# A third gate pair ahead of an output projection, more low parts by accumulating DMA, an earlier load: one layer of a streaming encoder on one core

## The chip, the cores and the metric

The kernel runs on 1 core of a Trainium2 chip. The metric is the time of one execution on the device in microseconds (us); lower is better. The core's engines work side by side, each on its own queue of instructions: TensorE (PE in the profile; its weight loads are PEld), VectorE (DVE), ScalarE (ACT), GpSimd (POOL) and SyncE (SP), which here only issues DMAs. DMAs are also issued from POOL's and ScalarE's queues.

## What is computed

One layer with three branches over a normed input, 512 prompt rows and 64 sample rows of width 1024 (576 columns in the kernel's transposed layout), all in float32:

```
h = rmsnorm(x);  proj = h @ w_in
glu_v, glu_g, conv_gate, z, xbc, dt, q, xa_gate, gates = split(proj)
A: u = glu_v * sigmoid(glu_g); c = causal depthwise conv of u, width 31
   out_a = (silu(layernorm(c)) * silu(conv_gate)) @ conv_out_w
B: state-space scan (SSD) over conv4(xbc) with dt, 4 groups of 8 heads
   y = y * silu(z); y = y * rsqrt(mean(y*y) per group) * ssd_norm_w
   out_b = y @ ssd_out_w
C: k, v = rmsnorm(mem) @ xa_kv_w          (256 memory rows)
   4 heads: o = softmax(q k' / 16) v;  out_c = (o * silu(xa_gate)) @ xa_out_w
m = sum over the branches of sigmoid(gates + gate_b) * out
y = x + rmsnorm(m @ w_out)
```

The sample rows attend to cached k and v and use cached conv and scan states. New caches and states are outputs too.

## The kernel before

**Products in three passes.** Each float32 operand is held as a high part and a low part (value minus high part), both in float32r. A product takes three matmuls: high by high, high by low, low by high (`mac`, L209 to L217). A projection (`proj`, L221) of 128 output channels over 576 columns has 8 chunks of the contraction, three passes and two column halves: 48 matmuls. The activation's parts, `hT`, stay in the core for the whole run.

**Weight jobs.** Weights come as jobs of 512 KB in a list, `order` (L95 to L165), in the sequence in which TensorE uses them. `prep_to` (L172) prepares job by job: SP loads `raw`; ScalarE writes the high part `whi` (L189); the low part `wlo` is made in one of two ways. For jobs ahead of `hold`, and for names that begin with k or v, VectorE subtracts (L191). For the others ScalarE writes the negated value (L193) and a DMA from POOL's queue adds `raw` onto it (L194). There are 3 buffers each of `raw`, `whi` and `wlo` in the pool `wp`. `W(name)` (L204) asks for the preparation of two jobs more (`LA`) than the one that it returns. `hold` marks where preparation stops until the attention is reached (`limit`).

**Stages.** (1) Norm and transposes of the input. (2) SSD, four groups of five chunks; the projections of the next things stand between the chunks as fill. (3) The end of group 3: `gating_a(3)` squares and sums y; then come the conv branch's gates `glu(0)`, the norm `gating_b(3)` (L644: two small matmul pairs, a square root, a reciprocal of 576 columns, four products L657, four splits into parts L616 and L618), `glu(1)`, sums for the next stage, and `out_b(3, q)`, which adds the last group's 192 matmuls onto `ob`. `glu(2)` stands behind it. A `glu` (L743) is two projections, a tanh into a tile `t`, and a product on VectorE into a padded tile `u` (`u_tile`), with small POOL copies (L736 to L740). (4) Paired products: 17 pairs of projections are done with seven products instead of eight on half blocks (`slot`, L950; P1 to P7, 84 matmuls a pair). The combinations T1 to T4 of the activation for it are formed ahead (L768 to L797) in tiles `xp` and `acc`. `pair_load`, `pair_pure` and `pair_sum` prepare weights; `pair_pure` uses the accumulating DMA (L877). Pair 0 and pairs 5 to 8 are gates of the conv branch, pairs 1 to 4 the merge gates of branch B, whose products end in `ob` and are stored to `msc` (L944), pairs 9 to 12 the attention's gates (stored to `spill["xg"]`), pairs 13 to 16 the merge gates of branch C. (5) Attention, head by head: `att_kq` projects k and q, `att_k` writes k out, `att_scores` projects v, writes it out and makes the scores and the softmax; the next head's `att_kq` stands between a head's scores and `att_pt` (transposes of the softmax, L1174) and `att_out`. (6) From 890 us: the output projection of C, layernorm, the branch A, the merges, `w_out`.

**Taps in the background.** The conv of width 31 is 8 channel tiles of a first product on ScalarE (L809) and 30 taps on VectorE (L816), queued in `bg`. `bgrun(n)` takes n of them from the queue. In the paired products it is called with 1 after every second slot; in the attention and later at fixed places.

**The memory rows** are loaded by SP into columns of `ob` (`obf`) that pairs 1 to 4 have stored, and normed in place (`mem_prep`, L1002), both called in the loop ahead of slot P5 of pair 8. The squares' output goes to columns 2048 to 3071 of the same tile.

**Who sets the order.** The program order is the source's, but the framework schedules: it simulates a time line with its own costs and lets ready instructions of an engine pass others, by a priority that follows the source order; `bgrun` shifts the priority of taps by 150. Each engine then runs its instructions strictly in the sequence fixed so. Waits between engines, and on buffers being freed, are put in by the framework.

## Time and profile before

| | us |
|---|---|
| runs | 1141.45, 1140.26, 1145.55 (median 1141.45) |
| profiled execution | 1143.13 |
| its span in the trace | 1141.4 |
| mean granted TensorE clock | 0.986 |
| TensorE busy | 1097.9 (96%) |
| VectorE busy | 868.8 (76%) |
| ScalarE busy | 606.4 (53%) |
| POOL busy | 148.3 (13%) |

A row of the windows gives, for a stretch of the span, each engine's busy time and instruction count, then the clock granted to TensorE (1.00 is full), the mean busy share of the 16 DMA engines, and GB/s. A row of the timeline gives start, duration, engine, source line, operation, output <- inputs, shapes, and in brackets the idle time before it with what ended it. A row of a group ends with busy time and the mean in ns of one instruction. A row of waits gives who waited for whom: us in total, times, longest.

### The profile page before, as it was taken

The page shows a single profiled execution, that of the slowest core. Times are in us where ns is not written, and L with a number is a line of the kernel's source. Part 1 is how long each engine was busy: PE and PEld are TensorE (multiplying, and loading weights), DVE is VectorE, ACT ScalarE, POOL GpSimd, SP SyncE. Part 2 cuts the span into 40 slices and gives each one's busy share as a digit, 9 for nine tenths or more (in the row PEclk, how much of TensorE's full clock was granted, in tenths as well). Part 3 has the DMA queues.
Part 4 walks back from the last instruction along what each step waited for, and adds up shares of the span by engine and source line. Part 5 has one row for each costly group of instructions (what it writes and reads, how often), then busy time and mean ns, then how long its engine had stood idle before and what let it go on. Part 6 is the DMA issues. An engine that isn't in the chain of part 4 may idle for free.

```text
span 1141.4 us, 20485 instructions
## 1 busy us (share of the span) xinstructions
PE 1097.9 (96%) x8081; PEld 1052.2 (92%) x8081; DVE 868.8 (76%) x1371; ACT 606.4 (53%) x1065; POOL 148.3 (13%) x237
## 2 busy tenths in 40 slices
PE   8999999999999999599989999899999999999997
PEld 8999999999999999599989999899898999999974
DVE  5778898488969886946787887389999998685433
ACT  5665655464537432535676666474457234685331
POOL 0100110020002100313224321000001011111000
PEclk9999999999999999799999999999999999999999
DMA  7354423442443323167887887666567786788812
GB/s 204 94 169 130 126 83 107 123 113 79 116 115 99 93 63 100 37 144 153 209 198 158 182 211 198 180 161 167 147 161 185 206 208 150 160 180 196 230 45 83
DMA packets 201495, 164.55 MB, mean 144 GB/s; under 512 B 14935, under 2 KB 175743, under 8 KB 201399
## 3 DMA queue, kind: packets, MB, share of 16 engines
q1 hardware_dynamic: 187142, 126.55, 38.8%
q0 software_dynamic: 13104, 34.35, 16.7%
q10 hardware_dynamic: 1152, 2.36, 0.5%
q8 instruction: 63, 1.03, 0.4%
q14 instruction: 34, 0.27, 0.1%
HBM read 114.85 MB, written 14.03 MB: 113 GB/s over the span
## 4 chain that ended last, share of the span: by engine, by line
PE 84%; DVE 7%; issue 3%; DMA 3%; ACT 2%; POOL 0%; DVEq 0%; SPq 0%; ACTq 0%; POOLq 0%
PE mm L214 55%; PE X L905 7%; DVE c L816 3%; PE Y L905 3%; PE ps L214 3%; PE Z L905 2%; PE ps L1114 2%; PE ps L1115 2%; PE ps L1113 2%; DMA pl<-rawb 2%; PE ps L573 2%; PE ps L599 2%; PE ps L577 1%; DVE wlo L191 1%; PE ps L538 1%
## 5 line engine op out<-in xcount | busy, mean ns | idle before, releaser
L214 PE MATMUL mm<-hT,whi 128*128 128x288 f32 (+2 forms) x2240 | 397.3, 297 | 1.0 <-ACT ob L668 0.5
L214 PEld LDWEIGHTS mm<-hT,whi 128*128 128x128 f32 x2240 | 334.3, 189 | 3.4 <-issue 1.3
L214 PE MATMUL mm<-hT,wlo 128*128 128x288 f32 (+2 forms) x1120 | 246.4, 298 | 0.0
L189 ACT ACTIVATE whi<-raw 128x1024 fp32r<-128x1024 f32 x118 | 124.8, 1057 | 216.2 <-PE mm L214 169.1
L816 DVE SCALAR_TENSOR_TENSOR c<-u,dww,c 128x606 f32<-128x606 f32 x240 | 199.6, 846 | 2.8 <-ACT c L809 0.3
L214 PEld LDWEIGHTS mm<-hT,wlo 128*128 128x128 f32 x1120 | 184.8, 189 | 1.3 <-issue 0.7
L191 DVE TENSOR_TENSOR wlo<-raw,whi 128x1024 fp32r<-128x1024 f32 x78 | 95.2, 1221 | 51.2 <-ACT whi L189 50.8
L214 PE MATMUL mm<-hi,whi 128*128 128x288 f32 x512 | 112.3, 301 | 10.8 <-DVE xs L657 10.8
L214 PE MATMUL mm<-lo,whi 128*128 128x288 f32 x512 | 111.4, 298 | 3.8 <-DVE lo L618 3.8
L214 PE MATMUL mm<-hi,wlo 128*128 128x288 f32 x512 | 110.9, 297 | 0.0
L214 PEld LDWEIGHTS mm<-hi,whi 128*128 128x128 f32 x512 | 83.3, 191 | 12.2 <-ACT hi L616 11.0
L214 PEld LDWEIGHTS mm<-lo,whi 128*128 128x128 f32 x512 | 83.3, 190 | 4.4 <-DVE lo L618 4.4
L214 PEld LDWEIGHTS mm<-hi,wlo 128*128 128x128 f32 x512 | 83.2, 189 | 0.2 <-issue 0.2
L194 POOL DMA_DIRECT2D wlo<-raw x40 | 34.7, 868 | 329.9 <-ACT wlo L193 257.4
L466 DVE SCALAR_TENSOR_TENSOR acc<-xp,scw,acc 128x579 f32<-128x579 f32 x72 | 58.3, 815 | 3.1 <-ACT acc L462 1.9
L193 ACT ACTIVATE wlo<-raw 128x1024 fp32r<-128x1024 f32 x40 | 42.0, 1049 | 27.8 <-PE ps L214 27.8
L888 DVE TENSOR_TENSOR wlo<-sm,whi 128x1024 fp32r<-128x1024 f32 x34 | 41.5, 1222 | 12.1 <-ACT whi L887 11.9
L875 ACT ACTIVATE ph<-rawb 128x512 fp32r<-128x512 f32 x34 | 21.4, 631 | 49.9 <-PE X L905 37.5
L877 POOL DMA_DIRECT2D pl<-rawb x34 | 29.9, 887 | 96.7 <-ACT pl L876 71.3
L458 POOL COPY tails<-xp 128x3 f32<-128x3 f32 x24 | 17.3, 720 | 193.3 <-ACT xp L456 187.8
L887 ACT ACTIVATE whi<-sm 128x1024 fp32r<-128x1024 f32 x34 | 35.8, 1055 | 11.4 <-PE X L905 7.5
L559 ACT ACTIVATE M<-R,tok 128x128 f32<-128x128 f32 (+1 forms) x80 | 24.8, 380 | 12.3 <-PE ps L599 12.3
(375 smaller groups left out, 2277.8 us busy)
## 6 DMA issues: line engine op xcount, KB each, us to landing
raw<-in_w_in_dram SPq DMA_DIRECT2D x70, 512.0 KB
wlo<-raw POOLq DMA_DIRECT2D x40, 512.0 KB, 5.7
raw<-in_w_in_dram SPq DMA_DIRECT2D x34, 256.0 KB
rawb<-in_w_in_dram SPq DMA_DIRECT2D x34, 256.0 KB
pl<-rawb POOLq DMA_DIRECT2D x34, 256.0 KB, 4.7
R<-scr SPq DMA_DIRECT2D x16, 512.0 KB
raw<-in_ssd_out_w_dram SPq DMA_DIRECT2D x16, 512.0 KB
raw<-in_xa_kv_w_dram SPq DMA_DIRECT2D x16, 512.0 KB
```

The source lines that it names most:

```text
L189: a = nc.scalar.activation(hi[:, :n_], raw[:, :n_], AF.Copy)
L191: b = nc.vector.tensor_tensor(lo[:, :n_], raw[:, :n_], hi[:, :n_].bitcast(F32), ALU.subtract)
L193: nc.scalar.activation(lo[:, :n_], raw[:, :n_], AF.Copy, scale=-1.0)
L194: nc.gpsimd.dma_start(out=lo[:, :n_], in_=raw[:, :n_], accum_op=ALU.add)
L214: m = nc.tensor.matmul(o, lhsT=w, rhs=r[:, s:s + w_], start=(i == 0 and a == 0), stop=(i == n - 1 and a == 2),)
L466: nc.vector.scalar_tensor_tensor(acc, xp[:, r:r + 579], w4[:, r, jt:jt + 1], acc, ALU.mult, ALU.add)
L559: nc.scalar.activation(M[:, 4 + e, :], R[:nl, 4 + e, :], AF.Relu, scale=-1.0, bias=tok[:nl, 0, c, a + 4:a + 5])
L816: nc.vector.scalar_tensor_tensor(c, upad[j][:, r:r + NC], w31[:, r, j:j + 1], c, ALU.mult, ALU.add)
L877: nc.gpsimd.dma_start(out=lo, in_=src, accum_op=ALU.add)
L887: nc.scalar.activation(hi, sm, AF.Copy)
L888: nc.vector.tensor_tensor(lo, sm, hi.bitcast(F32), ALU.subtract)
L905: nc.tensor.matmul(o, lhsT=w[:, k], rhs=r[:, k], start=(start and k == 0 and a == 0), stop=(k == 3 and a == 2), skip_group_check=True,)
```

## The change

- **Gates and q.** `glu(2)` moves from behind `out_b(3, .)` to behind `glu(1)`, with its tanh tile in the `acc` buffers. In its old place stand the projections q2 and q3, the q of head 1; ScalarE copies them to `bc` tiles and its queue stores them to a new scratch `spill["q"]`. In `att_kq(1)` they are loaded back by SP and split from there; the other heads project q as before.
- **Low parts.** The accumulating DMA makes the low part of every job from `gg0` on: the six gate jobs, the four out jobs of group 3, q2 and q3, and all k and v jobs.
- **Buffers and lead in the attention.** Of every five jobs from `hold` to the last v, two take their buffers from a new pool `wx` with 2 each of `raw`, `whi` and `wlo`; the lead there is four jobs instead of two, and three jobs instead of two are asked for at the start. The pool of T1 to T4 is closed ahead of that. `kk` (and `tu`, which shares it) has one buffer instead of two.
- **Memory.** The two loads get a function of their own, called ahead of P5 of pair 7; the norm is called ahead of P5 of pair 9.
- **Taps.** `bgrun(1)` after two slots of three.

```diff
-    for j in range(2):
+    for j in range(3):
         glu_jobs(j)
     for q in range(4):
         ob_job(3, q)
-    glu_jobs(2)
+    for i in (2, 3):
+        wjob(f"q{i}", w_in, C_Q + 128 * i)
     hold = len(order)
...
-            if h > 0:
+            if h > 1:
                 wjob(f"q{i}", w_in, C_Q + 128 * i)
...
-            raw = wp.tile([128, 1024], F32, tag="raw", name="raw", bufs=3)
-            hi = wp.tile([128, 1024], F32R, tag="whi", name="whi", bufs=3)
-            lo = wp.tile([128, 1024], F32R, tag="wlo", name="wlo", bufs=3) if name != "dt" else hi
+            wq, nb = (wx[0], 2) if hold <= nprep[0] <= pos["v3_1"] and nprep[0] % 5 > 2 else (wp, 3)
+            raw = wq.tile([128, 1024], F32, tag="raw", name="raw", bufs=nb)
+            hi = wq.tile([128, 1024], F32R, tag="whi", name="whi", bufs=nb)
+            lo = wq.tile([128, 1024], F32R, tag="wlo", name="wlo", bufs=nb) if name != "dt" else hi
...
-                if nprep[0] < hold or name[0] in "kv":
+                if nprep[0] < pos["gg0"]:
                     b = nc.vector.tensor_tensor(lo[:, :n_], raw[:, :n_], hi[:, :n_].bitcast(F32), ALU.subtract)
                 else:
                     nc.scalar.activation(lo[:, :n_], raw[:, :n_], AF.Copy, scale=-1.0)
...
-        prep_to(i + LA)
+        prep_to(max(i + LA, min(i + 4, pos["v3_1"])) if i >= hold else i + LA)
...
-        t = pool.tile([128, 640 if tag == "bc" else T], F32, tag=tag, name=tag, bufs=bufs)[:, 0:T]
+        t = pool.tile([128, T], F32, tag=tag, name=tag, bufs=bufs)
...
     glu(1, s2, "acc", 2)
+    glu(2, s2, "acc", 2)
...
     st.close()
-    glu(2, sx, "bc", 4)
+    for i in (2, 3):
+        pt = proj(f"q{i}")
+        t = sx.tile([128, 640], F32, tag="bc", name="bc", bufs=4)[:, 0:T]
+        nc.scalar.activation(v2(t), va(pt), AF.Copy)
+        nc.scalar.dma_start(out=spill["q"][i], in_=t)
...
+    def mem_load():
+        for t, (m_t, _) in enumerate(mt_):
+            nc.sync.dma_start(out=m_t, in_=mem_prompt[0, 128 * t:128 * t + 128])
+
     def mem_prep():
         for t, (m_t, _) in enumerate(mt_):
-            nc.sync.dma_start(out=m_t, in_=mem_prompt[0, 128 * t:128 * t + 128])
             rms_tile(m_t, 128, obf[:, 2 * D:3 * D], ssx[:, t], None)
 
     for i, (p, pr) in enumerate(seq):
-        if (p, pr) == (8, "P5"):
+        if (p, pr) == (7, "P5"):
+            mem_load()
+        if (p, pr) == (9, "P5"):
             mem_prep()
...
-        if i % 2:
+        if i % 3:
             bgrun(1)
...
     st.close()
+    stt.close()
     limit[0] = len(order)
-    prep_to(hold + LA - 1)
     st = ExitStack()
     keep = st.enter_context(tc.tile_pool(name="keep", bufs=2, reuse_waits="tile"))
     st3 = ExitStack()
+    wx.append(st3.enter_context(tc.tile_pool(name="wx", bufs=2, reuse_waits="tile")))
+    prep_to(hold + 2)
...
-    stt.close()
...
-        kk = a2.tile([128, 2, 256], F32, tag="kk", name="kk")
+        kk = a2.tile([128, 2, 256], F32, tag="kk", name="kk", bufs=1)
...
-            pt = q0[i] if h == 0 else proj(f"q{2 * h + i}")
-            nc.scalar.activation(v2(qhi[:, i]), va(pt), AF.Copy)
-            nc.vector.tensor_tensor(v2(qlo[:, i]), va(pt), v2(qhi[:, i].bitcast(F32)), ALU.subtract)
+            if h == 1:
+                src = sx.tile([128, 640], F32, tag="bc", name="bc", bufs=4)[:, 0:T]
+                nc.sync.dma_start(out=src, in_=spill["q"][2 + i])
+                src = v2(src)
+            else:
+                src = va(q0[i] if h == 0 else proj(f"q{2 * h + i}"))
+            nc.scalar.activation(v2(qhi[:, i]), src, AF.Copy)
+            nc.vector.tensor_tensor(v2(qlo[:, i]), src, v2(qhi[:, i].bitcast(F32)), ALU.subtract)
             bgrun(6)
```

More of the change, by code (lines that the diff above doesn't have):

```diff
@@ L90, in hybrid_trunk_kernel @@
     msc = dram.tile([8, 128, T], F32, name="msc")
-    spill = {k: dram.tile([8, 128, T], F32, name=f"spill_{k}") for k in ("xg", "g2")}
+    spill = {k: dram.tile([8, 128, T], F32, name=f"spill_{k}") for k in ("xg", "g2", "q")}
     scr = dram.tile([5, 32, 128], F32, name="scr")
@@ L170, in hybrid_trunk_kernel @@
     limit = [hold - 1]
+    wx = []
     def prep_to(n):
@@ L1224, in hybrid_trunk_kernel @@
             nc.tensor.transpose(p[:60, 128 * j:128 * j + 128], utail[:, 4 * b + j], ident)
-        tu = a2.tile([60, 512], F32, tag="kk", name="tu")
+        tu = a2.tile([60, 512], F32, tag="kk", name="tu", bufs=1)
         nc.scalar.activation(tu, p[:60, :], AF.Copy)
```

## The prediction

> **What bounds the kernel now.** I read the page first: the busy shares, then the slices.
>
> ```profile
> span 1141.4 us, 20485 instructions
> PE 1097.9 (96%) x8081; PEld 1052.2 (92%) x8081; DVE 868.8 (76%) x1371; ACT 606.4 (53%) x1065; POOL 148.3 (13%) x237
> PE   8999999999999999599989999899999999999997
> ```
>
> TensorE is the bound: 43.5 us of 1141.4 are idle, and only those, with the matmuls that run at a lowered clock beside them, can be won, since the change removes no matmul. The slices show one deep hole (slices 17 and 18). Next the stages, asked as windows (busy time and count of each engine, then TensorE's granted clock, DMA share, GB/s):
>
> ```profile
> 463.40:485.20 21.80, 8.82 (x49) 8.23 (x48) 21.68 (x28) 9.64 (x15) 10.95 (x10) 0.69 0.09 24
> 485.20:517.50 32.30, 32.28 (x242) 32.28 (x243) 15.71 (x19) 11.82 (x18) 3.67 (x4) 1.00 0.64 149
> 517.50:570.00 52.50, 51.59 (x388) 51.35 (x388) 39.51 (x60) 34.45 (x60) 16.60 (x18) 1.00 0.78 181
> 570.00:600.00 30.00, 25.93 (x178) 25.00 (x177) 24.41 (x37) 20.55 (x36) 6.10 (x8) 0.95 0.85 201
> 600.00:720.20 120.20, 116.63 (x865) 115.17 (x865) 93.10 (x138) 78.38 (x137) 33.93 (x36) 1.00 0.78 185
> 720.20:890.20 170.00, 159.47 (x1168) 151.91 (x1166) 147.56 (x228) 95.52 (x183) 9.49 (x11) 0.96 0.65 167
> 890.20:1080.00 189.80, 189.79 (x1423) 189.80 (x1424) 140.23 (x195) 93.16 (x115) 23.48 (x27) 1.00 0.81 190
> ```
>
> The reader is to see three places: the hole before the SSD's last output projection (463 to 485), a stall of 4 us in the paired products (570 to 600), and the attention (720 to 890), where VectorE is busy 147.56 of 170 us and TensorE idles 10.5. From 890 on TensorE has no gap, so a VectorE that finishes its taps sooner buys nothing there. Now the chain and the timeline around the hole:
>
> ```profile
> 485.22 32.27 PE mm L214 x240
> 462.98 0.43 PE L650 MATMUL ps<-tl,onesr 128*128 128x288 f32 x2
> 463.92 3.34 POOL L739 TENSOR_SCALAR utail<-u 128x30 f32<-128x30 f32 x1 [9.69 <-DVE u L751]
> 465.22 1.22 DVE L191 TENSOR_TENSOR wlo<-raw,whi 128x1024 fp32r<-128x1024 f32 x1
> 467.02 3.75 DVE L653 RECIPROCAL rs<-rs 128x576 f32<-128x576 f32 x1
> 474.21 1.33 PE L214 MATMUL mm<-hi,whi 128*128 128x288 f32 x4 [10.81 <-DVE xs L657]
> 477.69 0.85 PE L214 MATMUL mm<-lo,whi 128*128 128x288 f32 x2 [2.15 <-DVE lo L618]
> 477.76 6.00 POOL L737 COPY u<-sta 128x30 f32<-128x30 f32 x1
> 484.59 0.23 POOL L737 COPY u<-sta 128x30 f32<-128x30 f32 x1
> ```
>
> TensorE has finished the sum for group 3's norm and has nothing to do while VectorE goes through the reciprocal and the products with it (L657); then it restarts at a low clock (0.69 over this window).
>
> **Part 1: the third gate into the hole, two q projections behind.** A projection is 48 matmuls; 240 take 32.27 us, so one matmul 0.1345 and a projection 6.45. From 463.4 to 517.5 the kernel runs 49 + 242 = 291 matmuls, 39.1 us of work in 54.1: 15.0 are lost. The gate's 96 matmuls (12.9 us) go ahead of the out projection and keep TensorE busy to 476.3. The gating doesn't get later: it loses the low part at 465.22 (1.22 us) ahead of the reciprocal. So its first low part, which TensorE got at 477.69, should be there at about 476.3. Behind it run 192 matmuls of out projection and 96 of q: 387 in all, 52.1 us, so the paired products start at 515.5, only 2.0 earlier. The other 13.0 come back only if the attention, which no longer holds q2 and q3, gets shorter by their 12.9. Term: -15.0, of which 13 must be collected 200 us later. The evacuation of the two q (ScalarE copies, stores on ScalarE's queue) is put at nothing: ScalarE is busy 11.82 of 32.3 us there; without that cover it would cost 2 copies, each below the 1.05 us of a cast of 1024 columns (row in Part 2), so at most 2.1.
>
> The gate's tanh tile now comes from the buffers that the sums for T1 to T4 use, so these start later. Cover: VectorE has 16.6 us free from 485 to 517.
>
> **Part 2: low parts by accumulating DMA.** All six gate jobs, four out jobs and all k and v jobs leave VectorE. Rows: casts and low parts on the page, VectorE's share of the attention, and the issue and landing of the accumulates, first from 720 to 890, then from 890 to 1080.
>
> ```profile
> L189 ACT ACTIVATE whi<-raw 128x1024 fp32r<-128x1024 f32 x118 | 124.8, 1057 | 216.2 <-PE mm L214 169.1
> L193 ACT ACTIVATE wlo<-raw 128x1024 fp32r<-128x1024 f32 x40 | 42.0, 1049 | 27.8 <-PE ps L214 27.8
> wlo<-raw POOLq DMA_DIRECT2D x40, 512.0 KB, 5.7
> L191 DVE TENSOR_TENSOR wlo<-raw,whi 128x1024 fp32r<-128x1024 f32 x16 | 19.5, 1221 | 17.6 <-ACT whi L189 17.6
> L194 POOL DMA_DIRECT2D wlo<-raw x11: 859/859/877, 752.3 to 879.7; - x11
> DMA to landing us min/median/max: 4.5/4.6/7.3
> DMA to landing us min/median/max: 4.9/5.8/8.4
> ```
>
> A low part costs VectorE 1.22 us; now it costs ScalarE 1.05, POOL 0.86 and 5.7 to land, with the high part's 1.06 ahead about 8.7. In the hole the first out job's buffer comes free when gv1 ends (462.6). Cast and negated copy end at 464.8, POOL is held by the tail copy to 467.5, the part lands about 473.2, and TensorE wants it at 476.3: 3 us of slack. If POOL's op took 6.00 like the copy at 477.76, the slack is nearly gone. Bounds 0 to 2; I take +0.5.
>
> The two POOL copies above, of one form, took 6.00 us while VectorE was busy and 0.23 soon after. The Trainium skill, SBUF — State Buffer, section "Who interferes with whom", says: "A DVE instruction with two SBUF inputs contends with a GpSimd instruction that reads SBUF". The trace agrees for the copies; the accumulates' issues, 859 ns at the median beside a VectorE busy 87%, show no such delay. By the first reading the POOL work ahead of the out job's low parts stretches, and this term would be +2 rather than +0.5.
>
> In the attention VectorE loses 16 x 1.22 = 19.5 us. Most of that room is filled by taps that now lag behind 890, so it is no gain by itself. What it gives is shorter waits for VectorE, such as the 2.3 us for memT with a low part (1.22) just ahead of it. Bounds 0 to -10.5 (all idle time of the stage); I take -2, near the longest wait that TensorE's list names for VectorE in this stage:
>
> ```profile
> PE ps L331 <- DVE memT L334: 2.3, 1, 2.3
> ```
>
> ScalarE gets 16 x 1.05 = 16.8 us on 95.52 of 170: covered on average. POOL gets 16 x 0.86 on 9.49: covered. Each added ScalarE copy stands in order in front of the softmax's exponentials, which the next part prices. The DMA engines aren't covered so well. The queues over one head (738 to 775), with packets, MB and share:
>
> ```profile
> q1 hardware_dynamic: 7578, 4.67, 44.9%
> q0 software_dynamic: 288, 1.05, 15.2%
> SPq L179 <- DMA wlo<-raw: 205.0, 37, 18.6
> ```
>
> Two accumulates took 15.2% of 37 us, 2.8 each; 4.67 MB of loads took 16.6, so 512 KB 1.9. The stage has 0.65 x 170 = 110.5 us of DMA work. Add 16 x 2.8 = 45 and two reloads of q (2.1); take away q2's and q3's loads and accumulates (9.4): 148 us, in a stage that should last 157. That is 94%, above all that the windows show (0.85 at most). What waits is SP: its loads of raw weights wait for accumulates (last row), and behind them on the same queue stand the loads of q, of the caches and of the gates. Five buffers instead of three and a lead of four jobs cover a single late landing. Bounds: 0, if the engines take 94%, and +17, if they give no more than 0.85 (148/0.85 = 174 us). I take +2, near the lower end, since the 8.4 us of the longest landing is within four jobs' time (11.5 us by the k row of Part 3).
>
> **Part 3: the second head without its q.** Between head 0's scores and the transposes of its softmax TensorE has k2, q2, k3, q3 today:
>
> ```profile
> 755.53 0.69 PE L214 MATMUL mm<-hT,whi 128*128 128x288 f32 x4
> 756.22 2.88 PE ps L214 x24
> 765.69 0.49 ACT L1107 ACTIVATE P<-P,mx 64x256 f32<-64x256 f32 x1
> 774.06 1.04 PE L1174 MATMUL ps<-ident,P 128*128 128x128 f32 x8
> ```
>
> The scores end at 755.5, the softmax at 766.2, 10.7 later. Today's cover lasts to 774. With k2 and k3 alone (2.88 each) it lasts 5.8: a new hole of 4.9. It is 0 if the order lets head 1's v projection (48 such matmuls, 5.8 us) go first. I take +4: in today's order that projection stands behind the whole output of head 0.
>
> **Part 4: two taps in three slots.** Over the 119 slots 79 taps are issued instead of 59: 20 x 0.846 = 17 us of VectorE more.
>
> ```profile
> L816 DVE SCALAR_TENSOR_TENSOR c<-u,dww,c 128x606 f32<-128x606 f32 x240 | 199.6, 846 | 2.8 <-ACT c L809 0.3
> PE Y L905 <- ACT whi L887: 3.5, 2, 2.1
> ```
>
> VectorE goes from 157 to 174 of 202.7 us between 517.5 and 720.2, 77% to 86%. The longest named wait of the pairs is for ScalarE. Bounds 0 to +3.5, the size of that wait, should VectorE come to set another like it; I take +0.5. Nothing is won at the end, as the stage from 890 has no gap.
>
> **Part 5: the memory.**
>
> ```profile
> 567.11 0.34 SPq L1004 DMA_DIRECT2D ob<-in_mem_prompt_dram  x1
> 574.44 0.53 SPq L944 DMA_DIRECT2D msc<-ob  x1
> 580.00 1.06 ACT L270 ACTIVATE ob<-ob 128x1024 f32<-128x1024 f32 x1 [1.59 <-issue]
> 583.17 1.28 ACT L271 ACT_TABLE_LOAD   x1
> ```
>
> The second load already goes out at 567.11, 13 us before the squares at 580.00. The squares write over ob's columns 2048 to 3071, the last of which is ob 5, whose store to msc goes out at 574.44: that store holds them, not the load. So an earlier load wins nothing, and the squares with their table loads still stand in front of the pair's casts, which makes the waits for whi. The place costs 30 - 178 x 0.1345 = 6.1 us. Bounds -6 (the norm moves to where it hurts nobody) to +1; I take 0.
>
> kk's second buffer goes: a store of 256 KB (0.9 us by the rate above) would have to be late to cost anything; 0, at most +1.
>
> **Sum:** -15.0 + 0.5 - 2 + 2 + 4 + 0.5 + 0 = -10.0. The profiled execution took 1143.13 us, 1.7 beyond its span of 1141.4 and 1.7 above the median of the three runs; so 1133.1 for an execution like it, and 1131.4 for the median.
>
> **The rivals.** (a) More is won. The order fills head 1's hole (0 instead of +4), the norm moves out of the way (-4 instead of 0), DMA costs nothing (0 instead of +2), VectorE's waits shrink by 4 instead of 2: -22, 1119. For it: the hole's price is read from rows and the rest are small waits. Against it: the squares' wait for the store of ob 5, and the 4.9 us of missing cover.
>
> (b) The 13 us moved out of the attention aren't collected: the DMA engines stop at 0.90, 148/0.90 = 164 us instead of 157, +7 in place of +2, and the hole in head 1 comes in full with a restart at a low clock (2.2 us, as 8.82 - 49 x 0.1345 in the first window). Then -15 + 0.5 - 2 + 7 + 4.9 + 2.2 + 0.5 = -2: 1139. For it: the 94%. Against it: accumulates land in 4.6 us where VectorE is busiest.
>
> (c) Slower: DMA alone, at one place, 720 to 890. The longest stretch without a TensorE gap shows a share of 0.81. Were that the most the engines hold, the stage would last 148/0.81 = 183 us, 13 more than now, less the 2.0 of an earlier start: +11, 1152. It passes today's time once the share stays under 148/172 = 0.86. For it: no window of 30 us shows more than 0.85. Against it: at 0.81 TensorE was the bound, so this is demand, not a limit.
>
> (d) The memory part does nothing, by the rows above; that is in the sum.
>
> **How the numbers follow.** Changes under 0.5% (5.7 us) can't be told from none. Forecast, its own range 1124 to 1137: 0.50; (a) 0.22; (b) 0.16; (c) 0.12. Below 1135.7 lie (a), 0.46 of the forecast and 0.02 of (b): 0.70 faster. Within lie 0.04 and 0.14: 0.18. Slower: 0.12. The range of 1117 to 1144 takes in (a) and (b) and leaves out (c) and the far side of (a).
>
> **What would show it.** In the changed trace: between 463 and 485 a full TensorE at clock 1.00 and no wait for L657 over 2 us; the first paired product near 515.5; a wait before L1174 of about 4 us in head 1; the stage from q0 to the first oc projection at 161 us instead of 170, with a DMA share over 0.85 and VectorE still above 80%; the squares still behind the store of ob 5, and the waits for L887 still there; from there to the end no change. I am wrong if the out projection's first low part lands after 478, if TensorE waits in every head for weights, or if the pairs stall for VectorE.

## The result: slower, 1158.1 us against 1141.4

| | before | after |
|---|---|---|
| median of the runs (us) | 1141.4 | 1158.1 (1156.7 to 1161.7) |
| ratio to before, 95% interval | | 1.0144 [1.011, 1.0179] |
| span of the profiled execution | 1141.4 | 1154.7 |

All medians here and below leave out two slow runs, one of e1 (2046.2 us) and one of e16 (2722.1 us, its profiled one, so that e16 has no stages).

The page of the changed kernel, the same parts as were shown of before:

```profile
span 1154.7 us, 20551 instructions
PE 1100.2 (95%) x8081; PEld 1054.4 (91%) x8081; DVE 839.4 (73%) x1345; ACT 631.4 (55%) x1093; POOL 166.8 (14%) x263
PE   8999999999999999999989989588998899999997
PEclk9999999999999999999999999788999899999999
```

The hole, slice 17 of before (the prediction names 17 and 18, but 18 reads 9), is gone; there is a new one in slice 26, and TensorE's clock is lowered there. Windows in the cuts of the prediction, then finer ones (busy time of PE, PEld, DVE, ACT, POOL, clock, DMA share, GB/s; a DMA packet counts whole in the window in which it starts, so a share can pass 1):

```profile
463.40:485.20 21.80, 21.80 (x166) 21.80 (x165) 20.87 (x29) 15.02 (x20) 10.18 (x15) 1.00 0.62 141
485.20:517.50 32.30, 32.30 (x244) 32.30 (x244) 15.39 (x22) 15.26 (x22) 6.03 (x7) 1.00 0.94 204
570.00:600.00 30.00, 26.16 (x190) 24.99 (x189) 23.86 (x37) 23.90 (x42) 7.20 (x8) 1.00 0.77 191
720.20:890.20 170.00, 144.89 (x1049) 138.53 (x1049) 117.45 (x193) 97.11 (x181) 21.59 (x25) 0.91 0.85 201
720.00:740.00 20.00, 13.84 (x106) 13.60 (x104) 0.76 (x1) 5.10 (x8) 1.72 (x2) 0.95 1.07 269
740.00:760.00 20.00, 11.63 (x68) 10.46 (x69) 4.75 (x11) 11.98 (x21) 3.13 (x4) 0.67 0.77 170
880.00:900.00 20.00, 11.28 (x64) 9.36 (x62) 17.44 (x28) 7.93 (x18) 0.90 (x2) 0.87 0.79 202
```

Most of the loss stands in one stage. From 720.2 to 890.2 TensorE idles 25.1 us instead of 10.5, at a clock of 0.91 instead of 0.96, though 12.9 us of products (q2 and q3) have left the stage. VectorE, which was to be relieved, is busy 117.45 instead of 147.56; about 19 us of that are the 16 low parts that left, 11 are taps that ran elsewhere (99 instead of 111). TensorE's waits from 700 to 910:

```profile
PE ps L334 <- DVE memT L337: 12.6, 1, 12.6
PE mm L217 <- ACT hi L619: 6.9, 1, 6.9
PE mm L217 <- DMA wlo<-raw: 3.8, 3, 2.6
PE ps L217 <- ACT kk L1103: 2.4, 1, 2.4
PE ps L1193 <- ACT P L1121: 2.1, 1, 2.1
PE ps L1200 <- ACT P L1121: 2.1, 1, 2.1
```

(Lines of the changed kernel stand some further down: mac L217, casts L192, negated copies L196, accumulates L197, memT L336 and L337.) The longest names VectorE, but VectorE had nothing to do either. The chain of waits across that place:

```profile
720.66 9.32 DMA wlo<-raw
...
730.62 8.22 DMA raw<-in_xa_kv_w_dram
...
740.76 1.04 ACT whi L192
741.80 0.94 ACT wlo L196
742.75 0.94 ACT whi L192
743.69 0.95 ACT wlo L196
744.64 0.54 ACT qhi L1147
...
745.88 0.49 DVE memT L337
```

and ScalarE's own timeline:

```profile
728.25 0.63 ACT L1147 ACTIVATE qhi<-mm 128x576 fp32r<-128x576 f32 x1
738.85 1.06 ACT L192 ACTIVATE whi<-raw 128x1024 fp32r<-128x1024 f32 x1 [9.97 <-DMA raw<-in_xa_kv_w_dram]
744.55 0.63 ACT L1147 ACTIVATE qhi<-mm 128x576 fp32r<-128x576 f32 x1
745.08 1.55 ACT L336 ACTIVATE memT<-ps,vecs 128x256 fp32r<-128x256 f32 x4
```

So: an accumulate issued at 720.66 takes 9.3 us to land (before, the median was 4.6). It reads a raw tile, so SP can't load the next job into that buffer until 730. That load takes 8.2 us. ScalarE's next instruction is the cast of that job, a k job, whose product comes after 759; it waits 9.97 us for the load, and behind it stand two more casts, three negated copies, the q copy and the copies of the memory's transposes, without which TensorE can't go on. The q that ScalarE copies at 744.55 had been ready since 733. The Trainium skill, Perfetto Trace Analysis, section "Tensor Engine Instruction (MATMUL, LD_WEIGHTS)", says of ScalarE, VectorE and GpSimd that they are strict FIFO, while TensorE may pull weight loads ahead. The trace agrees: 11 us of ready work behind one late load. In before, one cast stands between the two q copies; its wait is for TensorE, not for a load, and the copies of memT stand right behind:

```profile
732.97 1.06 ACT L189 ACTIVATE whi<-raw 128x1024 fp32r<-128x1024 f32 x1 [4.80 <-PE mm L214]
734.46 1.56 ACT L333 ACTIVATE memT<-ps,vecs 128x256 fp32r<-128x256 f32 x4
```

To compare kernels, each span is cut at five points of its timeline: the start of the first product of the pairs, of the last one, of the first v product, of the first low part of oc (on VectorE), and the end.

| kernel (median us; ratio, interval) | pairs begin | pairs | start | heads | from oc | span |
|---|---|---|---|---|---|---|
| before (1141.4) | 517.3 | 202.8 | 19.0 | 150.3 | 252.0 | 1141.4 |
| after (1158.1) | 516.1 | 203.8 | 29.2 | 151.5 | 254.2 | 1154.7 |
| e1 (1142.2; 1.0004 [0.9984, 1.0024]) | 514.7 | 203.9 | 22.8 | 143.3 | 252.7 | 1137.3 |
| e2 (1137.3; 0.9964 [0.9947, 0.9981]) | 515.0 | 203.4 | 19.0 | 144.7 | 252.1 | 1134.3 |
| e3 (1128.6; 0.9873 [0.9852, 0.9895]) | 515.9 | 203.3 | 18.9 | 137.0 | 252.9 | 1128.0 |
| e4 (1139.0; 0.9962 [0.9947, 0.9977]) | 513.9 | 201.5 | 18.9 | 134.9 | 266.3 | 1135.5 |
| e5 (1157.8; 1.0139 [1.0119, 1.0159]) | 514.8 | 204.9 | 28.7 | 155.5 | 254.1 | 1157.9 |
| e6 (1156.5; 1.0127 [1.0104, 1.0149]) | 514.6 | 203.2 | 28.5 | 154.5 | 254.1 | 1155.0 |
| e7 (1129.1; 0.9886 [0.9866, 0.9905]) | 501.9 | 206.7 | 19.0 | 146.3 | 252.0 | 1126.0 |
| e9 (1135.2; 0.9927 [0.9901, 0.9953]) | 516.1 | 203.5 | 19.5 | 141.6 | 252.9 | 1133.5 |
| e10 (1139.2; 0.9995 [0.9973, 1.0017]) | 517.8 | 202.4 | 24.5 | 147.4 | 252.3 | 1144.3 |
| e11 (1198.3; 1.05 [1.0455, 1.0544]) | 514.4 | 203.7 | 29.1 | 195.6 | 254.3 | 1197.1 |
| e12 (1156.4; 1.0133 [1.0096, 1.017]) | 514.1 | 203.8 | 28.7 | 152.2 | 254.4 | 1153.3 |
| e13 (1128.7; 0.9891 [0.9861, 0.9921]) | 514.2 | 203.0 | 18.6 | 137.5 | 252.9 | 1126.3 |
| e14 (1147.7; 1.0046 [1.0029, 1.0063]) | 516.6 | 203.3 | 21.6 | 147.9 | 254.1 | 1143.5 |
| e15 (1136.1; 0.9944 [0.9927, 0.9961]) | 504.2 | 211.9 | 18.6 | 147.7 | 252.5 | 1135.0 |
| e17 (1123.7; 0.9841 [0.9812, 0.987]) | 503.4 | 207.2 | 14.8 | 147.9 | 253.6 | 1126.9 |
| e18 (1127.2; 0.9869 [0.9843, 0.9895]) | 514.9 | 202.4 | 14.8 | 139.3 | 252.3 | 1123.7 |

A profiled span lies up to 5 us from the median of its kernel (e10), so stages tell where, medians and ratios how much, and 2 us or less in one stage are at the edge of what can be read.

### The profile page after: what moved, and what is told of

Read it like the earlier page. It is cut to its first block, busy times and chain, and to the rows that moved or that the text cites. A ratio compares the mean times of both kernels' runs of the same rounds, so it can differ in the third digit from the quotient of the medians.

```text
span 1154.7 us, 20551 instructions
## 1 busy us (share of the span) xinstructions
PE 1100.2 (95%) x8081; PEld 1054.4 (91%) x8081; DVE 839.4 (73%) x1345; ACT 631.4 (55%) x1093; POOL 166.8 (14%) x263
## 5 line engine op out<-in xcount | busy, mean ns | idle before, releaser
L217 PE MATMUL mm<-hT,whi 128*128 128x288 f32 (+2 forms) x2240 | 399.2, 298 | 1.1 <-ACT ob L671 0.6
L217 PEld LDWEIGHTS mm<-hT,whi 128*128 128x128 f32 x2240 | 335.6, 189 | 3.7 <-issue 1.3
L217 PE MATMUL mm<-hT,wlo 128*128 128x288 f32 (+2 forms) x1120 | 248.1, 299 | 3.8 <-DMA wlo<-raw 3.8
L192 ACT ACTIVATE whi<-raw 128x1024 fp32r<-128x1024 f32 x118 | 124.7, 1057 | 209.5 <-PE mm L217 143.6
L217 PEld LDWEIGHTS mm<-hT,wlo 128*128 128x128 f32 x1120 | 185.5, 189 | 5.7 <-DMA wlo<-raw 4.6
L217 PE MATMUL mm<-hi,whi 128*128 128x288 f32 x512 | 112.4, 301 | 6.9 <-ACT hi L619 6.9
L197 POOL DMA_DIRECT2D wlo<-raw x66 | 57.5, 871 | 419.2 <-ACT wlo L196 370.1
L217 PE MATMUL mm<-lo,whi 128*128 128x288 f32 x512 | 111.4, 298 | 0.0
L217 PE MATMUL mm<-hi,wlo 128*128 128x288 f32 x512 | 110.9, 297 | 0.0
L217 PEld LDWEIGHTS mm<-hi,whi 128*128 128x128 f32 x512 | 83.4, 191 | 8.3 <-ACT hi L619 7.2
L194 DVE TENSOR_TENSOR wlo<-raw,whi 128x1024 fp32r<-128x1024 f32 x52 | 63.4, 1220 | 31.3 <-ACT whi L192 31.2
L217 PEld LDWEIGHTS mm<-hi,wlo 128*128 128x128 f32 x512 | 83.5, 190 | 0.0
L217 PEld LDWEIGHTS mm<-lo,whi 128*128 128x128 f32 x512 | 83.5, 190 | 0.0
L196 ACT ACTIVATE wlo<-raw 128x1024 fp32r<-128x1024 f32 x66 | 69.2, 1048 | 12.5 <-PE ps L217 11.5
L1271 DVE SCALAR_TENSOR_TENSOR lo<-lo,mm 128x576 f32<-128x576 f32 x8 | 6.0, 753 | 34.3 <-PE mm L217 34.3
```

Of the source, the lines that this page charges most:

```text
L192: a = nc.scalar.activation(hi[:, :n_], raw[:, :n_], AF.Copy)
L194: b = nc.vector.tensor_tensor(lo[:, :n_], raw[:, :n_], hi[:, :n_].bitcast(F32), ALU.subtract)
L196: nc.scalar.activation(lo[:, :n_], raw[:, :n_], AF.Copy, scale=-1.0)
L197: nc.gpsimd.dma_start(out=lo[:, :n_], in_=raw[:, :n_], accum_op=ALU.add)
L217: m = nc.tensor.matmul(o, lhsT=w, rhs=r[:, s:s + w_], start=(i == 0 and a == 0), stop=(i == n - 1 and a == 2),)
```

## Experiments

**e1, e2, e3: the lead and the accumulates, one and both taken back.** Before these ran the theory (A) was that ScalarE, which runs in a fixed order, is held by casts asked for four jobs ahead; the rival (B) that the accumulates are late or fill the DMA engines, a third (C) that the second head without its q is the cost.

```
e1, e3:  -  if nprep[0] < pos["gg0"]:
         +  if nprep[0] < pos["gg0"] or (nprep[0] >= hold and name[0] in "kv"):    # VectorE subtracts
e2, e3:  no pool wx, lead LA = 2 everywhere, prep_to(hold + LA - 1) at the start
```

> The changed kernel with the low parts of the 16 k and v jobs back on VectorE; the wider buffers and the lead of four jobs stay. Theory A (ScalarE's order: with a lead of four, casts stand ahead of the memory transposes and the softmax on ScalarE and wait there for weights; the weights wait on SP for accumulates) expects the 12.6 us wait before the memory transposes to fall below 5 us, since a raw buffer is free again 1.2 us after its cast, but casts to stay ahead of the softmax: about 1140. Theory B (the accumulates themselves, as DMA load and landing time, are the cost) expects everything lost in the attention back: 1130 to 1133, and a DMA share of 0.65 to 0.70 from 720 on. Theory C (the second head without its q is the cost, whatever makes the low parts) expects at most 5 us back: 1152 or more.

> The changed kernel without the pool of extra buffers and with a lead of two jobs as before; the k and v low parts stay with the accumulating DMA. Theory A expects most of the loss back, since the casts no longer stand so far ahead: 1140 or below, with no wait over 4 us before the memory transposes. Theory B expects no gain or a loss, since the same accumulates land with less cover: 1158 to 1175, with TensorE waiting for landings of low parts in every head. Theory C: 1153 to 1158.

> Both undone: k and v low parts on VectorE, lead of two, no extra pool; left are the gate and the two q ahead, the gates' low parts by DMA, the taps two in three and the memory load. All of the loss in the attention should be back but for head 1's missing cover (0 to 5 us): 1127 to 1133 by A and B. C expects 1145 or more, with one wait of 10 us or more in head 1.

Measured: 1142.2, 1137.3 and 1128.6. Each edit alone wins back a large part; with both undone the rest of the change is 1.3% faster than before, which rules out C (it expected 1145 or more). B missed both single edits (it expected 1130 to 1133 for e1, 1158 or more for e2). In the start the two are not additive: lead alone (e1) costs 3.9 us over e3, accumulates alone (e2) 0.1, both (after) 10.3. In the heads they are: 6.3 and 7.7, and 14.5 together. So neither A nor B alone is enough at the start.

**e5 and e6: the lead of the casts, and the lead at the start.** e5 lets the raw loads run four jobs ahead and asks for casts two ahead; e6 has the lead of four only from `v0_1` on.

```
e5:  +  load_to(max(nprep[0], min(i_lead[0], pos["v3_1"])) if nprep[0] >= hold else nprep[0])   # loads: i + 4
     +  prep_to(i + LA)                                                                         # casts: i + 2
e6:  -  ... if i >= hold else i + LA        +  ... if i >= pos["v0_1"] else i + LA
```

> The changed kernel (1158) with one thing taken apart: raw loads still go out four jobs ahead, into the five buffers, but the casts, the negated copies and the accumulates are issued only two jobs ahead. Theory A (a cast issued four jobs ahead stands in ScalarE's order in front of the copies TensorE waits for): the stalls around 733 to 747 and at the softmax shrink to those of the lead-two kernel, 1134 to 1140. Rival B (the raw loads are late, because they stand on SP's queue behind the accumulates that free their buffers, whatever the order of the casts): little changes, 1150 or more. If both are needed, something between, 1141 to 1149.

> The changed kernel with the lead of four only from v0_1 on; before it, at the start of the attention, the lead is two. Theory A says the stall at the start is one instance of a cost that recurs: the wait for memT falls from 12.6 to about 3 and the first v0 matmul comes at 741 instead of 749, so 1147 to 1151, and the rest of the lead's 21 us stays. Rival: the start is all of it (a cold beginning with all queues empty): 1136 to 1140. Rival: nothing but a shift, the time is lost again before the oc projections: 1155 or more.

Measured: 1157.8 and 1156.5, no change, with the start at 28.7 and 28.5 us. Taken as written this speaks for B. But ScalarE's timeline of e5 shows that the edit didn't reach what it was to test:

```profile
738.45 1.06 ACT L203 ACTIVATE whi<-raw 128x1024 fp32r<-128x1024 f32 x1 [9.77 <-DMA raw<-in_xa_kv_w_dram]
740.36 1.04 ACT L203 ACTIVATE whi<-raw 128x1024 fp32r<-128x1024 f32 x1
742.25 1.04 ACT L203 ACTIVATE whi<-raw 128x1024 fp32r<-128x1024 f32 x1
744.67 1.55 ACT L348 ACTIVATE memT<-ps,vecs 128x256 fp32r<-128x256 f32 x4
```

The same three casts stand ahead of memT. Where a request stands in the source doesn't fix the place; the framework's own time line does, and in it a cast is ready as soon as it counts a raw tile as loaded and a whi buffer as free. With five buffers it is ready early, with a lead of two in the source as with four; e10 tests this. e5's chain shows one more price of the loaded DMA engines, the single buffer of kk: in head 0 TensorE waits 8.7 us for a copy that waits for the store of the kk before it, 11.24 us on its way.

```profile
764.42 11.24 DMA out_dram<-kk
...
775.74 0.61 ACT kk L1116
```

**e10 and e14: ScalarE's sequence itself.** e10 is e5 with whi and wlo from the old three buffers alone; e14 is the changed kernel with the memory's transposes ahead of q0 and q1 in the source, and nothing else.

```
e10: -  wq, nb = (wx[0], 2) if hold <= nprep[0] <= pos["v3_1"] and nprep[0] % 5 > 2 else (wp, 3)
     +  wq, nb = wp, 3                         # whi, wlo; raw keeps five
e14: +  for j in range(8): tr_act(mt_, j, memT, V_MEM, NMEM)
        q0 = [proj(f"q{i}") for i in range(2)]
     -  for j in range(8): tr_act(mt_, j, memT, V_MEM, NMEM)
```

> The changed kernel with five raw buffers and raw loads four jobs ahead, but whi and wlo from the three buffers of the old pool alone, so that a cast can't be put more than three jobs ahead: in ScalarE's fixed order two casts (and their negated copies) less stand in front of the memory's copies. Accumulates, their number and the early loads stay. Theory A (order: the casts ahead of memT in ScalarE's queue make the stall): from the last paired product to the first v matmul 20 us instead of 29, and 1145 to 1150 in all. Rival B (loads late, held on SP's queue by accumulates, whatever stands behind them): 27 us or more there, and 1154 or more. Rival D (the DMA engines are full at 1.0 there): also no change.

> The changed kernel with the transposes of the memory rows (and their copies) ahead of the projections q0 and q1 in the source instead of behind them. Lead, buffers, loads, accumulates and their number are as in the changed kernel; only the sequence differs: four of the eight copies of memT now stand ahead of the casts of k and v jobs in ScalarE's queue, the other four among them. Theory (sequence fixed for loads that come late): the wait for memT falls from 12.6 us to under 5, the stretch from the last paired product to the first v product from 29 to 20 to 24, and 1149 to 1153 in all; the 14.5 us behind it stay. Rival B or D (loads or DMA engines, whatever the sequence): TensorE then waits for the weights of v instead, 28 us or more, 1156 or more.

Measured: e10 1139.2, 19 us less than after by the medians (10 by the spans), its start 24.5; e14 1147.7, 10 less, its start 21.6. Every accumulate is still there in both. e14's ScalarE does four of the eight copies of memT before any of these casts:

```profile
730.16 1.57 ACT L336 ACTIVATE memT<-ps,vecs 128x256 fp32r<-128x256 f32 x4 [8.75 <-DMA spill_g<-ct]
731.60 1.07 ACT L192 ACTIVATE whi<-raw 128x1024 fp32r<-128x1024 f32 x1
735.89 1.06 ACT L192 ACTIVATE whi<-raw 128x1024 fp32r<-128x1024 f32 x1 [1.73 <-DMA raw<-in_xa_kv_w_dram]
```

and its DMA engines are as full as in after, or fuller (the last three columns: clock, share, GB/s):

```profile
720.00:740.00 20.00, 15.45 (x116) 14.65 (x114) 3.29 (x7) 9.49 (x16) 2.60 (x3) 1.00 0.98 250
740.00:760.00 20.00, 15.55 (x95) 15.32 (x96) 9.37 (x15) 10.36 (x19) 3.45 (x4) 0.74 1.06 248
760.00:780.00 20.00, 16.25 (x127) 15.40 (x126) 18.24 (x32) 15.26 (x31) 3.45 (x4) 1.00 1.07 269
```

e14 changes the sequence alone and takes 7.6 of the 10.3 us out of the start. That is the shown cause of the start: a sequence fixed for loads that come early, and loads that come late. Full DMA engines alone don't make it; whether they cost part of what is left is not shown.

**e11: raw tiles not held by accumulates.** The accumulates of the attention's jobs read the weights from memory a second time, in two halves (shortened).

```
-  nc.gpsimd.dma_start(out=lo, in_=raw, accum_op=ALU.add)
+  for k2 in (0, kk // 2): nc.gpsimd.dma_start(out=lo[half], in_=<weights>[half], accum_op=ALU.add)
```

> The changed kernel with the accumulates of the attention's jobs reading the weights from memory a second time (in two halves each) instead of from the raw tile: raw buffers come free after ScalarE's two copies, and SP's loads don't wait for accumulates. ScalarE's order, with the early casts ahead of memT, stays the same as in the changed kernel, and so does the number of DMA bytes written. Theory A (order alone): 28 us or more from the last paired product to the first v matmul, 1153 or more. Rival B (the held buffers): 20 to 22 us there, 1143 to 1150. Both needed together (an order fixed for loads that come late): this one and the three-buffer one each cure the start. Rival D (DMA full): no change, or slower, 1158 or more.

Measured: 1198.3, slower by 40 than after. The wait for memT falls to 2.7, and the casts behind the q copy at 728.26 run with no wait for a raw tile (728.79, 730.69); but TensorE now waits for the low parts themselves (40.0 in the whole run, 7.0 of it before 800):

```profile
PE mm L226 <- DMA wlo<-in_w_in_dram: 40.0, 7, 15.9
...
PE ps L343 <- DVE memT L346: 2.7, 1, 2.7
```

With the buffers free the cast's wait of 9.97 us for a load is gone, so the held raw tile is one leg of that wait. The start is no shorter (29.1): q1's product is now late itself, and the copies of memT come at 743.52, hardly earlier than in after. So the expected 20 to 22 us of B didn't come, and as the edit puts a dearer transfer in, its total says nothing on A or B.

**e9: early loads without accumulates.** As e3, with raw loads four jobs ahead into five raw buffers, and two buffers for kk and tu.

```
+  load_to(max(nprep[0], min(i_lead[0], pos["v3_1"])) if nprep[0] >= hold else nprep[0])   # i_lead = i + 4; raw: wp 3, wx 2
+  wq, nb = wp, 3                                                                           # whi, wlo; casts i + 2
-  kk, tu: bufs=1      +  bufs=2
```

> The kernel with both undone, and on top of it raw loads of the attention four jobs ahead (five raw buffers, casts and low parts still two ahead), and two buffers again for kk and tu. If loads issued early help on their own: the 3 us of waits before whi or wlo that are left go, 1124 to 1127. If it is already bound elsewhere (P, memT, and the taps that end at 967): 1127 to 1130. If early loads take DMA from the cache and spill loads: 1131 or more.

Measured: 1135.2, 6.5 more than e3 instead of none; by the stages 4.6 of it are in the heads. The last of the three expected cases came. Which transfer the early loads hold up was not settled.

**e12: the tail tiles out of kk's buffer.**

```
-  tu = a2.tile([60, 512], F32, tag="kk", name="tu", bufs=1)
+  tu = a1.tile([128, 2, 256], F32, tag=("ck", "cv")[b], name="tu")...[:60]
```

> The changed kernel with the two tail tiles tu in the (by then idle) tiles of ck and cv instead of in the one buffer of kk. Theory: the 6.9 us for which TensorE waits for the first high part of oc at about 900 is the chain kk stored, tu copied, tu stored, tu copied on ScalarE in front of that part; without it 4 to 7 us go, with the lowered clock behind it up to 9: 1149 to 1154. Rival: the part stands behind the late cast of an out job and the late softmax in ScalarE's order, and the stores only fill that time: 1156 to 1159.

Measured: 1156.4, nothing that can be told from after. The wait for the first high part of oc falls from 6.9 to 1.3, and 3.1 for its low part and 8.4 for kk in head 0 (2.4 in after) come up. The second stands some 125 us ahead of the edited place, and e5 and e6 have it too (8.7 and 8.0), so whether the edit brought it is not shown, and with it whether the wait at the end cost anything.

**e4: the taps at every second slot again,** on e3.

```
-  if i % 3: bgrun(1)
+  if i % 2: bgrun(1)
```

> As the run before, with the taps back at every second slot. If the 2.3 us that the paired products lost (205 us instead of 202.7) come from the taps, it is 2 us faster in that stage; the 20 taps then run in the attention beside a VectorE that is full there, which may cost 0 to 3 us: 1127 to 1134, within 3 us of the run before.

Measured: 1139.0, 10 us slower than e3, against an expectation of 3 at most. The pairs do get 1.8 shorter and the heads 2.1; the stage from oc on gets 13.4 longer. The windows of e4 there, then those of e3:

```profile
1000.00:1020.00 20.00, 14.71 (x105) 14.12 (x103) 15.37 (x21) 15.58 (x19) 2.58 (x3) 0.90 0.62 142
1020.00:1040.00 20.00, 16.86 (x108) 15.66 (x108) 18.06 (x33) 10.78 (x14) 0.83 (x1) 0.93 0.29 80
```

```profile
1000.00:1020.00 20.00, 20.00 (x153) 20.00 (x151) 20.00 (x36) 17.24 (x23) 2.58 (x3) 1.00 0.73 164
1020.00:1040.00 20.00, 19.68 (x148) 19.45 (x147) 12.99 (x22) 11.61 (x15) 3.31 (x4) 1.00 0.73 165
```

and e4's chain through the layernorm, which stands on VectorE behind the taps (the last tap starts at 974.6, in e3 at 967.3):

```profile
1004.59 3.95 DVE mean L1302
...
1008.57 5.69 DVE u L1318 x8
1014.26 1.01 DVE u L1322 x2
```

**e7 and e15: q2 and q3 back in head 1, then the first low parts back on VectorE.** e7 is e3 with the two q projections where they were; e15 is e7 with the low parts of the gate and out jobs on VectorE too.

```
e7:  -  for i in (2, 3): wjob(f"q{i}", ...)   # ahead of hold, with their projections, stores and loads
     +  if h > 0: wjob(f"q{i}", ...)          # in head 1, as before
e15: +  if nprep[0] < hold or name[0] in "kv": # VectorE subtracts
```

> The kernel with both undone (1128.6: lead two, k and v low parts on VectorE) with q2 and q3 put back into head 1; the third gate stays ahead of the out projection. The two projections are 12.9 us of TensorE. Theory: the 13 us that the move was to collect are there once the attention runs as before, less what head 1 without its q costs, about 3 by its waits (2.5 for P, 1.3 for kf): 1136 to 1140. Rival of the prediction's Part 3 (a hole of 4.9 and a cold restart in head 1 without q): 1133 to 1136. Rival T (the taps, done at 967 of 1128, set the end): the 13 us would be mostly given back by the layernorm, 1128 to 1132.

> The kernel of e7 (both undone, q2 and q3 in head 1; 1129.1) with the low parts of the six gate jobs and the four out jobs on VectorE again as well: what is left of the change is the third gate in the hole, the taps and the memory. The prediction put the late low part of the out jobs at +0.5: if so 1128 to 1130. If VectorE's 12 us in front of the sums for T1 to T4 matter (e7 already starts the pairs with 3.5 us of gaps): 1130 to 1134.

Measured: e7 1129.1, the same as e3; the pairs begin 14.0 earlier, and the heads take 9.3 more, the pairs 3.4 more, so the move of q takes 9.3 of its 12.9 out of the heads and gains nothing in all. The theory's 1136 to 1140 missed; the number of rival T came without its reason, as the stage from oc on is only 0.9 longer in e3 than in e7. e15 1136.1, 7 more than e7: the pairs begin 2.3 later and take 5.2 more, with 5.6 us of waits for pl and 4.7 for ys (1.2 and 1.8 in e7). Between 463.4 and 485.2 and between 570 and 600, e7 first:

```profile
463.40:485.20 21.80, 21.80 (x166) 21.80 (x165) 20.89 (x31) 16.38 (x21) 10.30 (x16) 1.00 0.62 145
570.00:600.00 30.00, 27.30 (x198) 26.12 (x197) 25.61 (x40) 23.60 (x42) 11.17 (x10) 1.00 0.69 158
```

```profile
463.40:485.20 21.80, 20.81 (x152) 20.13 (x152) 19.53 (x24) 12.84 (x18) 7.42 (x12) 1.00 0.23 65
570.00:600.00 30.00, 23.50 (x150) 23.03 (x151) 21.67 (x34) 20.46 (x36) 5.93 (x8) 0.89 0.66 149
```

**e13: the memory's load and norm as before,** on e3.

```
-  mem_load() ahead of P5 of pair 7, mem_prep() ahead of P5 of pair 9
+  both in mem_prep() ahead of P5 of pair 8
```

> The kernel with both undone (1128.6) with the memory's load and norm again together ahead of P5 of pair 8. The prediction put this part at 0 (bounds -6 to +1): 1127.5 to 1130. If the earlier load, or the later norm, does bring what it could: 1131 to 1135.

Measured: 1128.7 against 1128.6. Nothing, as the prediction said.

**e16, e17, e18: a version that beats both.** e16 is e7 with the memory's transposes first and two buffers for kk and tu; e17 the same with one buffer; e18 has q2 and q3 ahead of the pairs and two buffers.

```
+  for j in range(8): tr_act(mt_, j, memT, V_MEM, NMEM)     # on e7 (e16, e17), on e3 (e18)
   q0 = [proj(f"q{i}") for i in range(2)]
-  kk, tu: bufs=1      +  bufs=2                            # e16, e18
```

> e7's kernel (1129.1) with the memory's transposes ahead of q0 and q1 and two buffers for kk and tu. The wait for memT is 2.3 us there, with a clock of 0.91 behind it: 1126 to 1128.5 if these go; 1128.5 to 1131 if another wait takes their place.

> e16's kernel (1123.2: both undone, q2 and q3 in head 1, the memory's transposes ahead of q0 and q1) with one buffer for kk and tu. If the transposes bring the 6 us: 1122 to 1125. If the buffers do (the prediction put them at 0 to 1): 1127 to 1130.

> The kernel with both undone (1128.6, q2 and q3 ahead of the paired products) with the memory's transposes ahead of q0 and q1 and two buffers for kk and tu. By the measured stages the move of q2 and q3 takes 9.3 us out of the attention and puts 12.9 ahead of it, and gets 3.5 back in the paired products: 1122 to 1125, as e16. If head 1 without its q costs more after a clean start: 1126 to 1129.

Measured: e16 1122.0, 0.9823 [0.9798, 0.9848] of before; e17 1123.7; e18 1127.2. e16 came out below both of its expected cases, e17 as expected, e18 in the slower of its two. The transposes first take the start from 19.0 to 14.8 (e7 against e17), and the wait for memT, 2.3 us in e7, is gone; the buffers bring nothing that can be told. The intervals of e17 and e18 overlap, and their spans stand the other way round (1126.9 and 1123.7), so whether the q should move stays open.

## Why the prediction was wrong

The sum was -10.0; the spans differ by +13.3. Set against its terms:

- **The hole, -15.0: right.** The window from 463.4 to 485.2 went from 8.82 to 21.80 busy at clock 1.00; the pairs began 1.2 earlier (2.0 forecast); e7, without the q there, begins them 15.4 earlier, of which 2.3 are the accumulates' (e15).
- **The head without its q, +4: right in size, not in place.** 12.9 us of products left and e3's heads got 9.3 shorter than e7's: 3.6. The wait was split between P (2.5 in e3) and smaller ones instead of 4 at one place.
- **VectorE's waits, -2: not collected.** The wait for memT that stood for it is 2.7 in e2, which has the accumulates and the old lead, against 2.3 in before. What takes it away is the order of the transposes (e17).
- **Part 2, the step that failed.** The prediction said: "Five buffers instead of three and a lead of four jobs cover a single late landing", took +2 for the DMA engines and put ScalarE down as "covered on average". The buffers did not cover the landing, they made it dear: they let casts pass ahead of copies that TensorE needs, each cast bound to a load, each load to an accumulate. Start and heads took 180.7 us, where 161 were forecast: 10 more in the start, and in the heads 14.5 over e3, of which the lead alone makes 6.3 (e1) and the accumulates alone 7.7 (e2). The prediction had both links (SP's loads wait for accumulates; ScalarE's copies stand in order) and priced neither, because it took an average busy share for a place in a queue, and said that the next part would price the copies, which it did not. That part was mis-sized by about 20 us. That the order of ScalarE's queue costs the time is shown for 7.6 us of the start (e14); for the heads only what each of the two edits is worth is shown.
- **Rival (c)** gave the nearest number, 1152, and the wrong reason. It held the DMA engines to a share of 0.81; e14 holds 0.98 to 1.07 over 60 us, and e10 and e14 win 10 to 19 us with every accumulate in place. So a limit of 0.81 is not what held the kernel; that loads take 8.2 us with the engines this full is part of the account, and what full engines cost beyond that stays open.
- **Low parts of gates and out jobs: wrong in sign.** +0.5 was taken for the late low part of the out jobs. The accumulates win 7 us there (e15 against e7), 5 of them in the pairs behind.
- **Taps, +0.5: within its bounds for the pairs, wrong for the end.** The pairs pay 1.8 (e4 against e3), hardly more than can be read. "Nothing is won at the end, as the stage from 890 has no gap" holds for a kernel whose attention ends at 890. In before the last tap starts at 973.3, in e4 at 974.6, but e4's attention ends 20 us earlier (869 against 889); TensorE's longest wait there is 5.1 us, at 1018.4, for the first high part behind the layernorm, and the stage is 13.4 longer than in e3. The gap that isn't there in a profile may be a margin that the change itself uses up.
- **Memory, 0: right** (e13; the squares still begin at 579.2, and the store of ob that ScalarE waits for lands at 579.1; the row of the timeline names a VectorE instruction before it). **kk's buffer, 0 to +1: right for a clean kernel** (e16, e17), too small for this one: TensorE waited 2.4 for it in after, and 8.7 in e5, where the store took 11.2 us to land.
- **From oc on, 0:** 2.2 longer in after. The products behind the wait of 6.9 us run at a granted clock of 0.50 from 900 to 904 and 0.85 to 908 (1.00 at that place in before), which is an estimate of 2 to 3 us.

What stays open: how the 14.5 us in the heads divide over single waits, and their cause. With the lead alone (e1) the longest is 8.1 before the first high part of oc, where e3 waits 1.1 for a low part; with the accumulates alone (e2) it is 4.8 for P, where e3 waits 2.5, and 3.1 for a low part. No run takes one of them out cleanly: e12, which removes the one of 6.9 in after, has others in its place.

## What to carry to other kernels

A queue that runs in a fixed order is as late as its latest entry: before giving a job a longer lead, look at what it will stand in front of, and at what its own input waits for. More buffers are not only slack; they are a permission for early work to go ahead of urgent work. And where an edit shortens a stage, ask what was due at the end of the old one: a stage without a gap can have been in balance by a few microseconds.

## What the runs showed of the hardware

- An accumulate of 512 KB landed later where more was moving: 4.6 us at the median in the attention of before (DMA share 0.65), 5.8 in the same stretch of after (0.85), 6.9 between 716 and 750 of after, where the two main queues take 50.3% and 39.3% of the engines:

```profile
q0 software_dynamic: 867, 3.16, 50.3%
q1 hardware_dynamic: 5817, 3.73, 39.3%
wlo<-raw POOLq DMA_DIRECT2D x6, 512.0 KB, 6.9
```

- Accumulating straight from the weights in memory, in halves, was dearer than from a tile in the core: from 750 to 880 of e11 8.52 MB took 50.6% of 130 us, 4.0 us of all engines for one of 512 KB (0.524 MB), against 3.0 in after (9.61 MB, 42.4% of 130 us).
- In the 20 us window in which the 12.6 us wait ends (740 to 760) TensorE's granted clock was 0.67. Two products of v took 0.63 us at 749.85 and 0.40 at 751.69, so the stall cost its length and slow matmuls behind it.
